# A hybrid SSD and gated-DeltaNet block on one core: kept decays, paired merges, reordered SSD chunks, and difference blocks made between products

## The chip, the cores and the metric

The kernel runs on 1 core of one Trainium2 chip. The metric is device time in microseconds of one execution (lower is better). The profile is one further execution, taken by the hardware profiler.

## The reference

The input x (1024 tokens of 1024 channels) gets 16 meta tokens ahead of it. One layer follows, in float32:

```python
h = h + hybrid_mixer(rmsnorm(h, mix_norm_w), ...)       # two token mixers side by side
h = h + swiglu(rmsnorm(h, ffn_norm_w), w_gate_up, w_down)
return rmsnorm(h, final_norm_w)[:, N_META:]
```

- `hybrid_mixer` projects with `w_in` to 13,376 columns. A causal convolution over 4 tokens and a SiLU make the inputs of the mixers.
- Mixer 1, Mamba-2 SSD: 32 heads of 64 channels in 4 groups, state 128. Per chunk: `scores = (C B^T) * exp(cumulative decay differences)`, `y = scores @ (x*dt) + decayed old state`, and a new state.
- Mixer 2, gated DeltaNet: 8 query/key heads, 16 value heads of 128. Per chunk: keys `k`, `a_low = strict lower part of (beta k k^T) * decay`, `t_inv = (I + a_low)^-1`, `v_new = u - w @ S`, `o = q_dec @ S + (q k^T * decay) @ v_new`, and a new state `S`.
- Both outputs are normed, gated (`silu(z)`), projected with `w_branch`, weighted by sigmoid gates, summed and projected with `w_out`.
- `swiglu` is `(silu(u @ Wg) * (u @ Wu)) @ Wd` with 2816 inner columns.

## The kernel before

Activations lie channels by tokens, 128 channels on the partitions. Every dense product is made of three matmuls in a reduced float32 format: each operand is split into a high and a low half (a copy on ScalarE, a subtraction on VectorE), and high x high, high x low and low x high are summed in PSUM (`dense`, L138 to L143; `product`, L1000 to L1004). `load_w` (L130 to L136) loads a weight tile into `wraw` (SyncE's queue), and splits it into `whi` and `wlo`; all three have two buffers. `weights(name)` (L192) loads one tile ahead, in the order of `proj_order`.

Stage 1, to about 80 us: norm of the input, decays of all heads (`cum`, `rowD`, `rowS`).

Stage 2, DeltaNet, to about 1090 us: eight head pairs (`NSUB`), one query/key head and two value heads each, chunks of 128 tokens, and a chunk of the 16 meta tokens (c = 8). Per pair i:
- `dn_conv(i)`: four weight tiles (q, k, v, v), convolution, and `squares` (L441): transposes of q and k to PSUM and a square with a sum on ScalarE, for the norms.
- `dn_p1(i, c)`: key-key product, `decay` (two broadcast matmuls L420, two Relu, one Exp), and the matrix `N` into `W`; `W` goes to DRAM in blocks of 32.
- `dn_inv(i)`: VectorE inverts all 32 x 32 diagonal blocks at once (60 operations), DMAs bring them back into `W`, transposed copies go to `T32`.
- `dn_merge(i, c)`: three steps of small matmuls (32 x 32, 32 x 64, 64 x 64 of the array; L567, L568, L574, L578) with copies between them join the blocks to the inverse of 128.
- `dn_p2(i, c)`: the recurrence. It makes `decay` a second time (L612), the query-key product (L610) and the transposed keys (L611), then the products with the state.
- Between them lie the z tiles of pair i - 1 and gate tiles: dense matmuls, 11 us each.

Stage 3, SSD, to about 1770 us: per group nine chunks (`ssd_chunk`, L690), spread over the weight tiles of the next group. Stage 4, to about 2160 us: branch products (`load_y`, `tile_`). Stage 5: `w_out`, then the FFN by a scheme with seven products instead of eight blocks: `head` (L1011) makes two of a tile's products, the loop over j (L1085) five, of sums and differences of weight blocks (`comb`, on GpSimd) with the blocks t1, t2, t3, 22, t4 of the normed activations. t1 to t4 and 22 are made ahead of the loop (L1066 to L1081). Then the down products and the final norm.

What sets the order: the text of the program gives priorities. A planner orders each engine's instructions when the program is built, from modelled durations, so dense matmuls of later tiles stand between the small ones of DeltaNet. Each engine then runs its list in that order and waits where an operand is not ready.

Of the kernel before, what the change touches and what calls it, by code (L numbers as in the profile page):

```python
# [20 lines left out]
NT = 1024  # L21
NM = 16
# [70 lines left out]
def body(tc, A):  # L93
# [35 lines left out]

    def load_w(src, kk=KD, room=None):  # L130
# [97 lines left out]
    convp = tkp.tile([128, len(CONV), 5], F32, name="convp")  # L228
    cvp = tc.tile_pool(name="cv", bufs=2)
# [201 lines left out]
    T32 = sb.tile([128, 16, 96], F32, name="T32", bufs=1)  # L431
    pool.memset(T32, 0.0)
    sub = [dict() for _ in range(NSUB)]

    def dn_conv(i):
        d = sub[i]
        qk = d["qk"] = sba.tile([128, 2, TT], F32, name="qk")
        ss = sb.tile([128, 2, 9], F32, name="ss")
        pool.memset(ss, 1.0)

        def squares(j):  # L441

            for cc in (range(4), range(4, 8), (8,)):
                ps = psm("z")
                for c in cc:
                    c0, L = cr(c)
                    pv = ps[0:L, 128 * (c % 4):128 * (c % 4) + 128]
                    pe.transpose(pv, qk[:, j, c0:c0 + L], ident)  # L448
                    act.activation(pv, pv, AF.Square, accum_out=ss[0:L, j, c:c + 1])
# [51 lines left out]
    def dn_p1(i, c):  # L501
        d = sub[i]
        c0, L = cr(c)
        if c == 8:
            d["W"] = sb.tile([128, 8, 2, 128], F32, name="W")
            d["Wm"] = sb.tile([NM, 2, NM], F32, name="Wm")
        kT = d["qk"][:, 1, c0:c0 + L]
        ps = psm("p")
        E = sb.tile([128, 2, 128], F32, name="E")
        pe.matmul(ps[0:L, 256:256 + L], kT, kT, start=True, stop=True)  # L510
        decay(E, ps, rowD, selD, 32, (2 * i, 2 * i + 1), c)
        kkm = sb.tile([128, 128], F32, name="kkm")
        dve.tensor_tensor(kkm[0:L, 0:L], ps[0:L, 256:256 + L], stri[0:L, 0:L], op=ALU.mult)
        N = d["W"][:, c] if c < 8 else d["Wm"]
        for h in range(2):
            dve.scalar_tensor_tensor(N[0:L, h], E[0:L, h, 0:L], d["w"][0:L, c, h:h + 1], kkm[0:L, 0:L],
                                     op0=ALU.mult, op1=ALU.mult)
        nd = nd_dram[i]
        if c in (3, 7):
            for b in range(4):  # L520
                r = slice(32 * b, 32 * b + 32)
                for h in range(2):
                    sp.dma_start(V(nd[0:64], "(c h b) s l -> s c h b l", h=2, b=4)[:, c - 3:c + 1, h, b],
                                 d["W"][r, c - 3:c + 1, h, r])
# [3 lines left out]
    def dn_inv(i):  # L528

        d = sub[i]  # L530
        X = sb.tile([66, 32, 32], F32, name="X", bufs=1)
# [18 lines left out]
        for b in range(3):  # L550
            r = slice(32 * b, 32 * b + 32)
            dve.transpose(T32[r, :, r], V(d["W"][r, :, :, r], "s c h l -> s (c h) l"))

    def dn_merge(i, c):

        d = sub[i]
        W = d["W"]
        ps = psm("p")
        zz = sb.tile([128, 2, 3, 32], F32, name="zz")
        p10 = sb.tile([64, 2, 32], F32, name="p10")  # L560
        z4 = V(ps[:, 0:192], "p (h b s) -> p h b s", h=2, b=3)
        for h in range(2):
            pe.matmul(ps[:, 96 * h:96 * h + 96], W[:, c, h], T32[:, 2 * c + h], start=True, stop=True)  # L563
        act.copy(zz, z4)
        p4 = V(ps[:, 192:256], "p (h s) -> p h s", h=2)
        for h in range(2):
            pe.matmul(p4[0:32, h], zz[32:64, h, 0], W[32:64, c, h, 32:64], start=True, stop=True)  # L567
            pe.matmul(p4[64:96, h], zz[96:128, h, 2], W[96:128, c, h, 96:128], start=True, stop=True)  # L568
            dve.transpose(p10[32:64, h], p4[0:32, h])
        act.copy(W[0:32, c, :, 32:64], p4[0:32])  # L570
        act.copy(W[64:96, c, :, 96:128], p4[64:96])
        p5 = V(ps[:, 256:320], "p (h s) -> p h s", h=2)
        for h in range(2):
            pe.matmul(p5[64:128, h], W[32:64, c, h, 64:128], p10[32:64, h], start=True, stop=True)  # L574
        dve.tensor_tensor(zz[64:128, :, 0], zz[64:128, :, 0], p5[64:128], op=ALU.add)
        p6 = V(ps[:, 320:448], "p (h s) -> p h s", h=2)
        for h in range(2):
            pe.matmul(p6[0:64, h], V(zz[64:128, h, 0:2], "p b s -> p (b s)"), W[64:128, c, h, 64:128],  # L578
                      start=True, stop=True)
        act.copy(W[0:64, c, :, 64:128], p6[0:64])  # L580

    def dn_meta(i):
        d = sub[i]
        kT = d["qk"][:, 1, 0:NM]
        ps = psm("a")
        pe.transpose(ps[0:NM, 0:128], kT, ident)
# [3 lines left out]
        kt = sb.tile([128, 128], F32, name="kt")  # L590
        vd = sb.tile([128, 2, 128], F32, name="vd")
        act.copy(kt[0:NM], ps[0:NM, 0:128])
# [3 lines left out]
        pe.matmul(ps[:, 0:256], kt[0:NM], V(vd[0:NM], "p h k -> p (h k)"), start=True, stop=True)  # L596
# [3 lines left out]
    def dn_p2(i, c):  # L600
# [3 lines left out]
        S, v, W = d["S"], d["v"], d["W"]  # L604
# [3 lines left out]
        ps = psm("b")  # L608
        E = sb.tile([128, 2, 128], F32, name="E2")
# [3 lines left out]
        qkm = sb.tile([128, 128], F32, name="qkm")  # L613
        kt = sb.tile([128, 128], F32, name="kt")
# [15 lines left out]
        for h in range(2):  # L630
            pe.matmul(pv[:, 128 * h:128 * h + 128], W[:, c, h], R[:, h], start=True, stop=True)  # L631
# [58 lines left out]
    def ssd_chunk(g, c):  # L690
# [17 lines left out]
        Bl = sb2.tile([128, 128], F32R, name="Bl")  # L708
        act.copy(Bh[0:L], ps[0:L, 0:128])
        dve.tensor_tensor(Bl[0:L], ps[0:L, 0:128], Bh[0:L], op=ALU.subtract)  # L710
        xh = sb2.tile([128, 512], F32R, name="xh", bufs=2)
        xl = sb2.tile([128, 512], F32R, name="xl", bufs=2)
        split(xh[0:L], xl[0:L], xde[0:L], dve)
        pst = psm("a")
        pe.matmul(pst, Bh[0:L], xh[0:L], start=True, stop=False)
        pe.matmul(pst, Bl[0:L], xh[0:L], start=False, stop=False)
        pe.matmul(pst, Bh[0:L], xl[0:L], start=False, stop=True)
        if c == 8:
            S = d["S"] = sb2.tile([128, 512], F32, name="Ss")
            act.copy(S, pst)  # L720
            return
        pe.matmul(ps[:, 128:256], Bc, Cc, start=True, stop=True)
        cbm = sb2.tile([128, 128], F32, name="cbm")
        dve.tensor_tensor(cbm, ps[:, 128:256], tri, op=ALU.mult)
        ec = sb2.tile([128, 4, 128], F32, name="ec")
        E = [sb2.tile([128, 4, 128], F32, name="Es", bufs=3) for _ in range(2)]
        for q in range(2):
# [6 lines left out]
            dve.tensor_tensor(E[q], E[q], cbm.unsqueeze(1).broadcast_to([128, 4, 128]), op=ALU.mult)  # L734
        S = d["S"]
# [68 lines left out]
    for i in range(NSUB):  # L804
# [136 lines left out]

    def sumsq(pl, sm, m, cs):
# [4 lines left out]
        q = pl.tile([128, 512], F32, name="sq")  # L947
# [47 lines left out]
    def raw_w(src, i):  # L995
        r = wp.tile([128, KD, 128], F32, name="wraw", bufs=2)
# [69 lines left out]
    for k in range(4):  # L1066
        norm(k, h2, rs2)
        dve.tensor_tensor(h[k][:, h1], h[k][:, h2], h[k][:, h1], op=ALU.subtract)
        put("t1", k, h[k][:, h1])
    for k in range(4):  # L1070
        norm(k + 4, h2, rs2)
        dve.tensor_tensor(h[k][:, h1], h[k + 4][:, h2], h[k][:, h1], op=ALU.subtract)
        put("t2", k, h[k][:, h1])
    for k in range(4):
        dve.tensor_tensor(h[k][:, h2], h[k + 4][:, h2], h[k][:, h2], op=ALU.subtract)
        put("t3", k, h[k][:, h2])
    for k in range(4):
# [162 lines left out]
```

## Time and profile before

| | |
|---|---|
| three runs | 2960.52, 2960.96, 2972.54 us (median 2960.96) |
| profiled execution | 2960.07 us; span from first to last instruction 2958.4 us |
| TensorE matmul (PE) | 2900.6 us busy, 98% |
| TensorE weight load (PEld) | 2442.0 us, 83% |
| VectorE (DVE) | 1971.9 us, 67% |
| ScalarE (ACT) | 1293.4 us, 44% |
| GpSimd (POOL) | 184.8 us, 6% |
| mean granted TensorE clock | 0.990 of full speed |

A matmul's end is modelled and matmuls overlap, so its own duration (0.39 us for 512 columns) is not what it costs; the distance to the next start is. L142 is a line of the kernel. "[0.24 <-issue]" behind a row is the engine's idle time ahead of it and what ended it.

### The profile page before, as it was taken

To read this page: it belongs to the slowest core of one execution; us is meant where nothing else is said; L and a number is where in the kernel's file an instruction comes from. 1 tells how busy PE (TensorE), PEld (TensorE's weight loads), DVE (VectorE), ACT (ScalarE), POOL (GpSimd) and SP (SyncE) were. 2 spreads that over 40 slices of the span, in tenths; PEclk is the share of its full clock that TensorE was granted. 3 is DMA by queue.
4 is the path that set the end of the run, shared out by engine and by line. 5 is a ranking of instruction groups with operands and counts; after the bars stand their busy time and mean duration, and the time that the engine had idled before them with its cause. 6 is when DMAs were issued, how large, how long until landed. Compare 5 with 4: busy or idle time off the path is not lost.

```text
span 2958.4 us, 42844 instructions
## 1 busy us (share of the span) xinstructions
PE 2900.6 (98%) x16121; PEld 2442.0 (83%) x16121; DVE 1971.9 (67%) x3882; ACT 1293.4 (44%) x3240; POOL 184.8 (6%) x193
## 2 busy tenths in 40 slices
PE   8999999999999999999999999999997999999997
PEld 7888888888888889979888778888876788888886
DVE  7678687787786755767777753564768655556446
ACT  5645545546456353545555544122234233333213
POOL 1000000000000000000000000000101432230000
PEclk9999999999999999999999999999998999999998
DMA  3111121120111201011111124352442222226212
GB/s 114 51 51 44 41 61 44 37 65 27 53 58 30 93 29 51 30 67 47 51 45 45 68 76 154 106 178 90 135 160 86 102 83 86 86 85 224 90 54 75
DMA packets 119255, 227.33 MB, mean 77 GB/s; under 512 B 47064, under 2 KB 53880, under 8 KB 119048
## 3 DMA queue, kind: packets, MB, share of 16 engines
q1 hardware_dynamic: 117320, 222.50, 22.7%
q8 instruction: 127, 2.08, 0.3%
q10 hardware_dynamic: 1728, 2.10, 0.2%
q14 instruction: 80, 0.66, 0.1%
HBM read 175.16 MB, written 49.38 MB: 76 GB/s over the span
## 4 chain that ended last, share of the span: by engine, by line
PE 91%; DVE 4%; DMA 2%; issue 1%; ACT 1%; POOL 1%; SPq 0%; DVEq 0%; ACTq 0%; POOLq 0%
PE psd L142 16%; PE psd L141 16%; PE psd L143 16%; PE pq_p L1002 1%; PE pq_p L1003 1%; PE ps_o L748 1%; PE pq_p L1004 1%; PE ps_p L563 1%; PE pq_psd L1002 1%; PE ps_o L641 1%; PE ps_z L448 1%; PE pq_psd L1003 1%; PE pq_psd L1004 1%; PE ps_a L631 1%; PE ps_b L738 1%
## 5 line engine op out<-in xcount | busy, mean ns | idle before, releaser
L142 PE MATMUL psd<-u_lo,whi 128*128 128x512 f32 (+3 forms) x2136 | 766.2, 359 | 3.7 <-DVE u_lo L150 2.7
L141 PE MATMUL psd<-u_hi,whi 128*128 128x512 f32 (+3 forms) x2136 | 761.1, 356 | 0.0
L143 PE MATMUL psd<-u_hi,wlo 128*128 128x512 f32 (+3 forms) x2136 | 754.9, 354 | 0.7 <-DVE wlo L135 0.7
L134 ACT CAST whi<-wraw 128x1024 fp32r<-128x1024 f32 (+2 forms) x197 | 188.0, 954 | 634.8 <-PE psd L142 454.3
L142 PEld LDWEIGHTS psd<-u_lo,whi 128*128 128x128 f32 x2136 | 406.2, 190 | 40.5 <-issue 5.1
L143 PEld LDWEIGHTS psd<-u_hi,wlo 128*128 128x128 f32 x2136 | 403.9, 189 | 33.0 <-issue 3.3
L141 PEld LDWEIGHTS psd<-u_hi,whi 128*128 128x128 f32 x2136 | 402.6, 189 | 34.6 <-issue 4.2
L135 DVE TENSOR_TENSOR wlo<-wraw,whi 128x1024 fp32r<-128x1024 f32 (+2 forms) x197 | 217.8, 1106 | 138.8 <-ACT whi L134 129.5
L143 PE MATMUL psd<-blk,wlo 128*128 128x512 f32 x512 | 199.4, 389 | 0.8 <-DVE wlo L135 0.8
L141 PE MATMUL psd<-blk,whi 128*128 128x512 f32 x512 | 199.2, 389 | 0.0
L142 PE MATMUL psd<-blk,whi 128*128 128x512 f32 x512 | 199.2, 389 | 0.0
L143 PEld LDWEIGHTS psd<-blk,wlo 128*128 128x128 f32 x512 | 96.1, 188 | 21.6 <-DVE wlo L135 1.7
L141 PEld LDWEIGHTS psd<-blk,whi 128*128 128x128 f32 x512 | 96.1, 188 | 20.0
L142 PEld LDWEIGHTS psd<-blk,whi 128*128 128x128 f32 x512 | 96.1, 188 | 19.8
L908 DVE TENSOR_TENSOR part<-part,psd 128x512 f32<-128x512 f32 x96 | 65.5, 683 | 70.2 <-PE psd L143 70.2
L378 ACT COPY raw<-psd 128x256 f32<-128x256 f32 x165 | 73.4, 445 | 81.9 <-PE psd L143 80.1
L379 POOL MEMSET raw<- 128x3 f32 x56 | 6.3, 113 | 1393.0 <-DVE qk L384 537.1
L986 POOL TENSOR_TENSOR sw<-wraw 128x512 f32<-128x512 f32 x44 | 69.3, 1575 | 353.1 <-DMA wraw<-w_gu 345.1
L702 DVE TENSOR_TENSOR xdt<-ps_z,dtb 128x512 f32<-128x512 f32 (+1 forms) x36 | 24.8, 690 | 89.0 <-PE ps_z L699 89.0
L539 DVE TENSOR_TENSOR itmp<-X 66x30 f32<-66x30 f32 (+14 forms) x240 | 78.2, 326 | 6.3 <-DMA X<-nd 0.8
L541 DVE TENSOR_TENSOR X<-X,itmp 66x30 f32<-66x30 f32 (+14 forms) x240 | 78.3, 326 | 5.9
L423 ACT ACTIVATE Es<-ps_p,cum 128x128 f32<-128x128 f32 x256 | 75.4, 371 | 11.0 <-PE ps_p L420 10.9
(678 smaller groups left out, 6145.3 us busy)
## 6 DMA issues: line engine op xcount, KB each, us to landing
wraw<-w_in SPq DMA_DIRECT2D x105, 512.0 KB, 3.3
wraw<-w_gu SPq DMA_DIRECT2D x48, 512.0 KB, 3.3
wraw<-w_br SPq DMA_DIRECT2D x36, 512.0 KB, 3.4
c<-hc SPq DMA_DIRECT2D x22, 512.0 KB, 2.6
hc<-c SPq DMA_DIRECT2D x22, 512.0 KB, 5.7
wraw<-w_dn SPq DMA_DIRECT2D x40, 256.0 KB, 2.6
g<-zt SPq DMA_DIRECT2D x32, 256.0 KB, 2.0
y_d<-zt SPq DMA_DIRECT2D x32, 256.0 KB, 2.1
```

What stands on the lines that cost most here:

```text
L134: act.copy(hi[:, 0:kk], raw[:, 0:kk])
L135: dve.tensor_tensor(lo[:, 0:kk], raw[:, 0:kk], hi[:, 0:kk], op=ALU.subtract)
L141: pe.matmul(ps[:, 0:n], hi[:, wk0 + k], ahi(k), start=(k == 0), stop=False)
L142: pe.matmul(ps[:, 0:n], hi[:, wk0 + k], alo(k), start=False, stop=False)
L143: pe.matmul(ps[:, 0:n], lo[:, wk0 + k], ahi(k), start=False, stop=(k == kk - 1))
L378: dense_u((name, lambda ps, p0, p1: act.copy(raw[:, 3 + p0:3 + p1], ps)))
L423: act.activation(E[0:L, i, 0:L], ps[0:L, 128 * i:128 * i + L], AF.Relu, bias=cum[0:L, c, h0 + h:h0 + h + 1], scale=-1.0)
L539: dve.tensor_tensor(t, X[:, 0:j, j:j + 1].broadcast_to([66, j, m]), X[:, j:j + 1, j + 1:32].broadcast_to([66, j, m]), op=ALU.mult)
L541: dve.tensor_tensor(X[:, 0:j, j + 1:32], X[:, 0:j, j + 1:32], t, op=ALU.add)
L908: dve.tensor_tensor(part[:, m, cs], part[:, m, cs], ps, op=ALU.add)
L986: pool.tensor_tensor(t, x, y, op=op)
L1002: pe.matmul(ps, w[0][:, k], y[0][:, k], start=start and k == 0, stop=False, skip_group_check=not start)
```

## The change

1. DeltaNet, decays kept: `dn_p1` also makes the query-key product, and `E` (decay times masked query-key) is kept for all eight chunks (`bufs=8`); `dn_p2` makes neither decay, nor that product, nor the transposed keys. The keys are copied out of the transposes of `squares` (two copies of four chunks, `kt`), and `squares` makes a group's transposes first and its squares behind them.
2. DeltaNet, paired merges: `dn_merge` joins two chunks at once (four heads per step). `W` becomes two halves of four chunks (three buffers), its blocks return with 16 DMAs instead of 8; `T32` shares a buffer with `X` and is cleared in each pair.
3. SSD chunks: B, C and the decays first, then x; the state products and the new state behind the y products.
4. `wraw` has one buffer up to the end of the SSD stage (pool `wr1`), then two (`wr2`).
5. FFN: each of the five blocks is made just ahead of the first product that uses it; for j = 0 `comb` runs on VectorE.
6. End: the last norm's scaling is one VectorE operation per tile for all columns; output DMAs go by SyncE's queue, but for odd tiles of the last columns; the squares have two buffers.

```diff
-        raw = wp.tile([128, KD, 128], F32, name="wraw", bufs=2)
+        raw = raws[0].tile([128, KD, 128], F32, name="wraw")
...
                 for c in cc:
-                    pe.transpose(pv, qk[:, j, c0:c0 + L], ident)
-                    act.activation(pv, pv, AF.Square, accum_out=ss[0:L, j, c:c + 1])
+                    pe.transpose(pv(c), qk[:, j, c0:c0 + L], ident)
+                if j == 1 and len(cc) > 1:
+                    d["kt", cc[0] // 4] = kt = sb.tile([128, 4, 128], F32, name="kt", bufs=3)
+                    act.copy(kt, V(ps, "p (c k) -> p c k", c=4))
...
+                for c in cc:
+                    act.activation(pv(c), pv(c), AF.Square, accum_out=ss[0:cr(c)[1], j, c:c + 1])
...
-        ps = psm("p")
+        ps = psm("pb"[c % 2])
         pe.matmul(ps[0:L, 256:256 + L], kT, kT, start=True, stop=True)
+        if c < 8:
+            pe.matmul(ps[:, 384:512], kT, qT, start=True, stop=True)
+            E = d["E", c] = sb.tile([128, 2, 128], F32, name="E", bufs=8)
...
+            dve.tensor_tensor(qkm, ps[:, 384:512], tri, op=ALU.mult)
...
+            dve.tensor_tensor(E, E, qkm.unsqueeze(1).broadcast_to([128, 2, 128]), op=ALU.mult)
...
-                sp.dma_start(d["W"][r, :, h, r], bv(xd_dram[i])[:, :, h, b])
+                for k in range(2):
+                    sp.dma_start(d["W"][k][r, :, h, r], bv(xd_dram[i])[:, 4 * k:4 * k + 4, h, b])
...
+        ch = [(c + h // 2, h % 2) for h in range(4)]
+        for h, (k, e) in enumerate(ch):
+            pe.matmul(ps[:, 96 * h:96 * h + 96], W[:, k, e], T32[:, 2 * k + e], start=True, stop=True)
+        act.copy(zz, V(ps[:, 0:384], "p (h b s) -> p h b s", h=4, b=3))
...
+        dve.transpose(V(p10[32:64], "p h s -> p (h s)"), ps[0:32, 384:512])
...
-        pe.matmul(ps[:, 256:384], kT, qT, start=True, stop=True)
-        pe.transpose(ps[:, 384:512], kT, ident)
-        decay(E, ps, rowD, selD, 32, (2 * i, 2 * i + 1), c)
-        dve.tensor_tensor(qkm, ps[:, 256:384], tri, op=ALU.mult)
-        act.copy(kt, ps[:, 384:512])
-        dve.tensor_tensor(E, E, qkm.unsqueeze(1).broadcast_to([128, 2, 128]), op=ALU.mult)
+        E, kt = d.pop(("E", c)), d["kt", c // 4][:, c % 4]
...
+        x, xdt, xh, xl = inputs()          # ssd_chunk: behind both decay tiles
         S = d["S"]
...
+        pst = states(xh, xl)               # behind the y products
         dve.tensor_tensor(t1, t1, j4(py), op=ALU.add)
+        S2 = d["S"] = sb2.tile([128, 512], F32, name="Ss")
+        dve.tensor_tensor(h8(S2), h8(S), bc(clast), op=ALU.mult)
+        dve.tensor_tensor(S2, S2, pst, op=ALU.add)
...
+    def block_product(ps, w, y, start):
+        if blocks:
+            blocks.pop(0)()
...
+        product(ps, w, Y[y], start, True)
...
+        eng = pool if j else dve
...
-            product(pc, parts(s1, slot()), Y["t1"], True, True)
+            block_product(pc, parts(s1, slot()), "t1", True)
...
-                    if c == 512:
-                        dve.scalar_tensor_tensor(x, x, finw[:, k:k + 1], rs, op0=ALU.mult, op1=ALU.mult)
-                    else:
-                        act.activation(x, x, AF.Copy, scale=finw[:, k:k + 1])
-                        (pool if k % 3 == 1 else dve).tensor_tensor(x, x, rs, op=ALU.mult)
-                    (sp, act)[k // 2 % 2].dma_start(A["out"][:, k, cs], x)
+                    dve.scalar_tensor_tensor(x, x, finw[:, k:k + 1], rs, op0=ALU.mult, op1=ALU.mult)
+                    (act if cs.stop == NT and k % 2 else sp).dma_start(A["out"][:, k, cs], x)
```

## Rows read from the trace of the kernel before

**Rows 1.** Busy by window: PE, PEld, DVE, ACT, POOL, clock, DMA share, GB/s.

```profile
80.00:1090.00 1010.00, 1008.57 (x6477) 854.23 (x6476) 760.76 (x2083) 546.34 (x1812) 14.50 (x49) 0.99 0.16 49
...
261.00:303.00 42.00, 42.00 (x245) 36.70 (x244) 39.59 (x96) 19.57 (x54) 0.42 (x4) 1.00 0.16 54
```

**Rows 2.** Timeline of TensorE in DeltaNet: start, duration, line, shape, count.

```profile
566.80 0.39 PE L631 MATMUL ps_a<-v,W 128*128 128x128 f32 x2
567.11 0.65 PE L574 MATMUL ps_p<-p,W 32*64 32x32 f32 x8
567.69 0.49 PE L610 MATMUL ps_b<-qk 128*128 128x128 f32 x2
568.01 0.27 PE L611 MATMUL ps_b<-ident,qk 128*128 128x128 f32 x1
568.12 0.28 PE L420 MATMUL ps_b<-rowD,selD 96*128 96x128 bf16 x2
568.21 0.48 PE L142 MATMUL psd<-u_lo,whi 128*128 128x512 f32 x1
568.52 0.39 PE L143 MATMUL psd<-u_hi,wlo 128*128 128x512 f32 x1
568.75 0.38 PE L641 MATMUL ps_o<-v,E 128*128 128x128 f32 x2
```

**Rows 3.** Timeline of TensorE: first and last of the 211 merge visits.

```profile
196.32 0.21 PE L567 MATMUL ps_p<-W,zz 32*32 32x32 f32 x1
...
1074.15 0.44 PE L578 MATMUL ps_p<-W,zz 64*64 64x64 f32 x4
```

**Rows 4.** Timeline of TensorE: a transpose of the squares between dense matmuls.

```profile
272.07 0.33 PE L448 MATMUL ps_z<-ident,qk 128*128 128x128 f32 x1
272.15 0.42 PE L142 MATMUL psd<-u_lo,whi 128*128 128x384 f32 x1
272.41 0.34 PE L143 MATMUL psd<-u_hi,wlo 128*128 128x384 f32 x1
272.59 0.33 PE L141 MATMUL psd<-u_hi,whi 128*128 128x384 f32 x1
```

**Rows 5.** Waits: who for whom, us in total, times, longest.

```profile
PEld ps_z L448 <- ACT ps_z L449: 23.8, 99, 0.4
```

**Rows 6.** Timeline of TensorE: first and last of the 57 y visits.

```profile
1198.01 0.66 PE L748 MATMUL ps_o<-Es,xdt 128*64 128x128 f32 x8
...
1737.44 0.66 PE L748 MATMUL ps_o<-Es,xdt 128*64 128x128 f32 x8
```

**Rows 7.** VectorE's groups in DeltaNet: count, busy us, mean ns, idle before.

```profile
L617 DVE TENSOR_TENSOR E<-E,qkm 128x256 f32<-128x256 f32 x64 | 26.8, 419 | 2.0 <-ACT E L426 0.7
...
L615 DVE TENSOR_TENSOR qkm<-ps_b,tri 128x128 f32<-128x128 f32 x64 | 18.4, 287 | 4.9 <-ACT E L423 4.1
```

**Rows 8.** One line's instructions: duration ns min, median, max.

```profile
L548 SPq DMA_DIRECT2D W<-xd x64: 318/448/644, 187.7 to 1029.7; - x64
```

**Rows 9.** Timeline of TensorE where the FFN starts.

```profile
2288.78 0.80 PE L1004 MATMUL pq_psd<-tx,ws_wr 128*128 128x512 f32 x1 [10.33 <-DVE ws_wr L992]
...
2309.16 0.63 PE L1004 MATMUL pq_p<-tx,ws_whi 128*128 128x512 f32 x1
```

**Rows 10.** Timeline of VectorE where the FFN starts.

```profile
2252.45 3.35 DVE L186 RECIPROCAL rs<-rs 128x512 f32<-128x512 f32 x1 [0.70 <-ACT rs L185]
...
2279.61 4.29 DVE L150 TENSOR_TENSOR blk<-hc,blk 128x512 fp32r<-128x512 f32 x7
```

**Rows 11.** Timeline of ScalarE at the end.

```profile
2941.44 0.42 ACT L948 ACTIVATE sq<-hc 128x256 f32<-128x256 f32 x1 [3.78 <-DMA out<-hc]
```

**Rows 12.** Timeline of SyncE's queue: three weight loads.

```profile
1120.20 23.06 SPq L133 DMA_DIRECT2D wraw<-w_in  x3
```

**Rows 13.** Timeline of ScalarE: the split that follows.

```profile
1129.23 1.05 ACT L134 CAST whi<-wraw 128x1024 fp32r<-128x1024 f32 x1 [3.03 <-PE psd L142]
```

**Rows 14.** DMA issues of the page: count, KB each, us to landing.

```profile
wraw<-w_in SPq DMA_DIRECT2D x105, 512.0 KB, 3.3
```

More of the change, by code (lines that the diff above doesn't have):

```diff
@@ L437, in dn_conv @@
         qk = d["qk"] = sba.tile([128, 2, TT], F32, name="qk")
+        d["ktm"] = sb.tile([NM, 128], F32, name="ktm")
         ss = sb.tile([128, 2, 9], F32, name="ss")
@@ L554, in dn_merge @@
+        pool.memset(T32, 0.0)
+        for k in range(2):
+            for b in range(3):
+                r = slice(32 * b, 32 * b + 32)
+                dve.transpose(T32[r, 8 * k:8 * k + 8, r], V(d["W"][k][r, :, :, r], "s c h l -> s (c h) l"))
     def dn_merge(i, c):
         d = sub[i]
-        W = d["W"]
+        W, T32 = d["W"][c // 4], d["T32"]
+        T32 = T32[:, 8 * (c // 4):8 * (c // 4) + 8]
+        c = c % 4
+        ch = [(c + h // 2, h % 2) for h in range(4)]
         ps = psm("p")
-        zz = sb.tile([128, 2, 3, 32], F32, name="zz")
@@ L560, in dn_merge @@
[L560 to L574, printed above, removed]
+        zz = sb.tile([128, 4, 3, 32], F32, name="zz")
+        p10 = sb.tile([64, 4, 32], F32, name="p10")
+        for h, (k, e) in enumerate(ch):
+            pe.matmul(ps[:, 96 * h:96 * h + 96], W[:, k, e], T32[:, 2 * k + e], start=True, stop=True)
@@ new lines, in dn_merge @@
+        act.copy(zz, V(ps[:, 0:384], "p (h b s) -> p h b s", h=4, b=3))
+        c4 = lambda t: V(t, "p (k e) s -> p k e s", e=2)
+        p4 = V(ps[:, 384:512], "p (h s) -> p h s", h=4)
+        for h, (k, e) in enumerate(ch):
+            pe.matmul(p4[0:32, h], zz[32:64, h, 0], W[32:64, k, e, 32:64], start=True, stop=True)
+            pe.matmul(p4[64:96, h], zz[96:128, h, 2], W[96:128, k, e, 96:128], start=True, stop=True)
+        dve.transpose(V(p10[32:64], "p h s -> p (h s)"), ps[0:32, 384:512])
@@ L575, in dn_merge @@
+        act.copy(W[0:32, c:c + 2, :, 32:64], c4(p4[0:32]))
+        act.copy(W[64:96, c:c + 2, :, 96:128], c4(p4[64:96]))
+        ps = psm("p")
+        p5 = V(ps[:, 0:128], "p (h s) -> p h s", h=4)
+        for h, (k, e) in enumerate(ch):
+            pe.matmul(p5[64:128, h], W[32:64, k, e, 64:128], p10[32:64, h], start=True, stop=True)
         dve.tensor_tensor(zz[64:128, :, 0], zz[64:128, :, 0], p5[64:128], op=ALU.add)
-        p6 = V(ps[:, 320:448], "p (h s) -> p h s", h=2)
-        for h in range(2):
-            pe.matmul(p6[0:64, h], V(zz[64:128, h, 0:2], "p b s -> p (b s)"), W[64:128, c, h, 64:128],
+        p6 = V(ps[:, 128:384], "p (h s) -> p h s", h=4)
@@ L579, in dn_merge @@
+        for h, (k, e) in enumerate(ch):
+            pe.matmul(p6[0:64, h], V(zz[64:128, h, 0:2], "p b s -> p (b s)"), W[64:128, k, e, 64:128],
                       start=True, stop=True)
-        act.copy(W[0:64, c, :, 64:128], p6[0:64])
+        act.copy(W[0:64, c:c + 2, :, 64:128], c4(p6[0:64]))
     def dn_meta(i):
         d = sub[i]
-        kT = d["qk"][:, 1, 0:NM]
         ps = psm("a")
-        pe.transpose(ps[0:NM, 0:128], kT, ident)
         for h in range(2):
@@ L589, in dn_meta @@
                       start=True, stop=True)
-        kt = sb.tile([128, 128], F32, name="kt")
+        kt = d["ktm"]
         vd = sb.tile([128, 2, 128], F32, name="vd")
-        act.copy(kt[0:NM], ps[0:NM, 0:128])
         dve.tensor_tensor(vd[0:NM], V(ps[0:NM, 128:384], "p (h k) -> p h k", h=2),
@@ L595, in dn_meta @@
         ps = psm("a")
-        pe.matmul(ps[:, 0:256], kt[0:NM], V(vd[0:NM], "p h k -> p (h k)"), start=True, stop=True)
+        pe.matmul(ps[:, 0:256], kt, V(vd[0:NM], "p h k -> p (h k)"), start=True, stop=True)
         S = d["S"] = sb.tile([128, 2, 128], F32, name="S", bufs=3)
@@ L630, in dn_p2 @@
         for h in range(2):
-            pe.matmul(pv[:, 128 * h:128 * h + 128], W[:, c, h], R[:, h], start=True, stop=True)
+            pe.matmul(pv[:, 128 * h:128 * h + 128], W[:, h], R[:, h], start=True, stop=True)
         vd = sb.tile([128, 2, 128], F32, name="vd")
@@ L995, in raw_w @@
     def raw_w(src, i):
[L996 removed]
+        r = raws[0].tile([128, KD, 128], F32, name="wraw")
         sp.dma_start(r, src)
```

154 lines of the change are left out of this document (87 added, 67 removed).

## The prediction

> **What bounds the kernel now.** I read the busy shares of the page's table first: TensorE is at 98%, so a change has to take time out of TensorE's own stream, or out of the few places where that stream stands still. The windows say where it stands [rows 1]: in the DeltaNet stage (80 to 1090 us) it idles 1.4 us of 1010. But a busy matmul is a modelled one, so the third view, the matmuls in order of time, is read for the distance from one start to the next [rows 2]. The matmul of 512 columns at 568.52 costs 0.23 us; the one before it, of the same size, costs 0.31, because other work ran just ahead of it. Such small losses are what the change can reach in the first two stages. In the window of an inverse VectorE is full as well, busy 39.59 of 42 us [rows 1], which comes back as a rival. Real idle time stands in two short places: where the FFN starts (10.33 us ahead of one matmul, [rows 9]) and at the very end.
>
> **DeltaNet: kept decays.** Each of the 64 steps (8 head pairs, 8 chunks) loses one transpose and two decay broadcasts on TensorE. In [rows 2] the transpose L611 takes 568.12 - 568.01 = 0.11 us, the two broadcasts L420 568.21 - 568.12 = 0.09. So 64 x 0.20 = 12.8, and the eight meta transposes, at the same 0.11, make 0.9: 13.7 us. The query-key product moves to the first pass and costs the same there. It stood in a visit of its own; without the visit the dense matmul behind no longer pays its 0.31 - 0.23 = 0.08. 64 x 0.08 is 5; as some visits lie against other work of the same chunk, I take 3 (0 to 5). ScalarE loses two Relu, an Exp and a copy per chunk; it isn't the bound, so nothing is counted.
>
> **DeltaNet: squares.** Today a key or query transpose waits until ScalarE has squared the one before, in the same bank: 99 such waits [rows 5]. In [rows 4] the dense matmul behind one costs 0.26, the next, of the same size, 0.18. With four transposes in a row only the last one's follower pays: 96 of 128 followers x 0.08 = 8, and of each wait as much again at most. I take 10 (0 to 14).
>
> The Trainium skill (TensorEngine Tiling (Array Packing), Key Properties) says that changing the tiling mode drains TensorE, and that changing the tile alone does not. Full-size transposes change no mode, so by that rule this term would be nil and the sum 10 us smaller; the row shows a loss without a change of mode, and I go by the row.
>
> **DeltaNet: paired merges.** The matmuls stay the same in number; what halves is how often the array goes from full size to small tiles and back. In [rows 2] the two full-size L631, 0.11 each as L611, take 0.31 to the first small one: going in costs 0.09. Behind the eight small L574 the two L610 take 0.32 instead of 0.22: 0.10. That is 0.19 a visit, and what the way out takes itself, which these rows don't separate. I counted the uninterrupted visits of lines 567 to 578 in the timeline: 211, from the first to the last of [rows 3]. Paired, three steps in 32 pairs make 96; the planner now splits some of its 192, so I expect about 110. 100 visits fewer x 0.18 (some touch each other) = 18 us. Bounds: 5 if half the pairs are split again, 27 if each visit saved 0.27.
>
> What it costs: the second pass waits for both chunks' merge, while the four heads' transposes on VectorE become one. Dense matmuls lie beside it; if they run out, that is the third rival.
>
> DeltaNet together: 13.7 + 3 + 10 + 18 = 45 us.
>
> **SSD order.** Decays first, then x. Today the y products of a chunk come in two visits of eight instructions, 57 visits for 32 chunks [rows 6]. With both decay tiles ready before x, one visit per chunk: 25 fewer, at 0.19 and some way out, 0.26: 7 us. The state products move behind y and the new state behind them; the next chunk wants it only a tile later. Bounds -3 (the state comes late) to 10.
>
> **FFN start.** Today VectorE makes all five difference blocks before the first product can end: TensorE waits 10.33 us until 2288.78, and the five products of j=0 end at 2309.16 + 0.4 [rows 9], 20.8 us for 60 matmuls that need 60 x 0.23 = 13.8, as GpSimd is late with the combinations. Afterwards j=0 is paced by VectorE's list: from the reciprocal's end, 2252.45 + 3.35 = 2255.8, 44 block operations (12, 12, 8, 4, 8) and about 15 others (low halves, combinations, additions) at 4.29 / 7 = 0.61 us [rows 10]: 59 x 0.61 = 36, to 2291.8; the last product ends 12 x 0.23 = 2.8 later, 2294.6. Gain 15 us. Bounds: 4 if most blocks are still placed first (of the 7 us lost on GpSimd some are saved), 22 if combinations and halves run before the reciprocal ends.
>
> **End.** ScalarE sat 3.78 us behind output DMAs that it issues itself and that wait for VectorE [rows 11], and it scales a tile between two squares. Both go; one VectorE operation with both factors replaces the work of two or three engines. I take 3 (1 to 5).
>
> **One raw buffer for w_in.** The next tile's load now waits until the tile before is split. Today's load starts then already: at 1120.20 [rows 12] a load is issued, the next split starts at 1129.23 [rows 13], 9 us later; landing takes 3.3 [rows 14]. Hidden with 5.7 us to spare: cost 0, at the start of the kernel up to one landing, 3.3. With that cover gone a tile would cost 3.3 us.
>
> The Trainium skill (Trainium Kernel Development and Optimization, Best Practices) asks for double buffers, so that DMA and compute overlap. By that rule the 103 later tiles would pay their 3.3 us, 340 in all, and the time would be 3230; in the rows above the overlap comes from the split halves, which keep two buffers, so I give that 1 in 100.
>
> **Sum.** 45 + 7 + 15 + 3 = 70 us, from the profiled execution's 2960.07 (span 2958.4, and 1.7 around it): 2890. The median of the runs, 2960.96, is 1 us from it, so the same number stands. All low ends: 13.7 + 0 + 0 + 5 - 3 + 4 + 1 - 3 = 18, time 2942; all high ends: 13.7 + 5 + 14 + 27 + 10 + 22 + 5 = 97, time 2863.
>
> **Rivals.**
> 1. *The visits are split as before.* The order on each engine is the planner's, and it makes 57 y visits of a possible 32 today. Merges and y then give nothing: 2890 + 18 + 7 = 2915. For it: [rows 6]; against it: all operands of a paired step come ready with one copy. 0.17.
> 2. *The FFN blocks still come first,* as VectorE's list is ordered before it runs: 2890 + 11 = 2901. Against it: each block now stands behind the halves of its own product. 0.15.
> 3. *The chain of dependences governs DeltaNet (the slower side).* An inverse cannot start before the first pass is done, and that pass gets two more VectorE products per chunk, 0.287 + 0.419 us [rows 7], 64 x 0.706 = 45 us; behind the inverse 64 more DMAs are issued, 0.448 each [rows 8], 29 us. If no dense matmuls are left to lie beside them, 74 us come on top, nothing of DeltaNet's 45 is gained, and the time is 2960 + 74 - 7 - 15 - 3 = 3009. It decides once the dense work runs out inside a head pair. For it: VectorE full during the inverse. Against it: TensorE idles 1.4 us in the whole stage, so dense work has lasted everywhere, and the second pass is rid of the same two products. 0.05.
> 4. *Half of it:* DeltaNet's saved TensorE time becomes time only by half, as VectorE is full beside it: 2890 + 22 = 2912. 0.15.
>
> My forecast, all terms within their bounds: 0.45; mixtures of 1, 2 and 4, near 2945: 0.02; the single buffer 0.01. About 0.5%, 15 us, is what a measurement can tell from no change. Slower by more: 0.06 (rival 3 and the single buffer). Within: 0.04, the mixtures and the worst of rival 4. Faster: 0.90, all the rest. Range 2862 to 2930: below it lies more than all high ends, above it rival 3, the mixtures and the worst ends of 1 and 4.
>
> **What would show it.** L420 gone from the second pass; merge visits near 110 and y visits near 32; few waits of TensorE's weight loads for the squares; j=0 of the FFN done 15 us sooner after the reciprocal than today; no wait of ScalarE for output DMAs. I am wrong if TensorE shows waits of a microsecond and more inside DeltaNet, or if the splits of w_in wait for a DMA.

## The result and the profile after

The changed kernel takes 2935.72 us (median of 4 runs, 2933.44 to 2938.23) against 2961.86 for the one before: a ratio of 0.9904, 95% interval 0.988 to 0.9929. The sign is the forecast one, the size is not: 26 us came where 70 were forecast, and 2935.7 lies above the range.

The span of the profiled executions fell by 24.6 us, from 2958.4 to 2933.8. By stage, cut at the starts of four TensorE instructions that both kernels have (last products of the second pass, last SSD norm transpose, first and last FFN product):

| stage | before | after | gain | forecast |
|---|---|---|---|---|
| start and DeltaNet | 1088.8 | 1081.1 | 7.6 | 45 |
| SSD | 706.3 | 702.5 | 3.9 | 7 |
| branch and w_out | 452.0 | 451.2 | 0.8 | 0 |
| FFN | 446.1 | 438.3 | 7.9 | 15 |
| down and end | 265.2 | 260.7 | 4.4 | 3 |

DeltaNet hands over more than its end says: dense w_in matmuls worth 638.2 us (each counted at its undisturbed price, 0.23 us for 512 columns) are done by then, against 630.4. So DeltaNet gained 7.6 + 7.8 = 15.4 us, and SSD, which finds 7.8 us less to do, lost 4.

The windows of the changed kernel (busy us and count of PE, PEld, DVE, ACT, POOL, then clock, DMA share, GB/s) answer to [rows 1]: all of DeltaNet, its last 161 us, and a stretch inside them.

```profile
80.00:1081.00 1001.00, 964.77 (x6310) 841.29 (x6309) 733.09 (x1979) 464.08 (x1446) 24.51 (x56) 0.99 0.17 50
920.00:1081.00 161.00, 144.84 (x935) 116.95 (x934) 98.63 (x311) 61.90 (x216) 2.37 (x3) 0.95 0.15 47
943.00:992.00 49.00, 32.84 (x223) 25.48 (x222) 36.57 (x140) 24.09 (x99) 0.94 (x1) 0.89 0.09 23
```

Before, TensorE idled 1.4 us of 1010 here. Now it idles 36 of 1001, and 16 of the 49 us from 943 to 992, where the timeline has no dense matmul between these two:

```profile
948.31 0.39 PE L145 MATMUL psd<-u_hi,wlo 128*128 128x512 f32 x1
992.41 0.78 PE L143 MATMUL psd<-u_hi,whi 128*128 128x512 f32 x1
```

No other engine is full there. The waits of TensorE in DeltaNet (who for whom, us in total, times, longest) answer to [rows 5]:

```profile
PE psd L143 <- ACT raw L382: 10.2, 15, 1.7
PE ps_z L692 <- DVE zt L402: 6.9, 3, 4.5
PE ps_o L661 <- ACT v L657: 3.8, 5, 1.0
PE ps_b L524 <- DVE rs_to L163: 2.3, 1, 2.3
...
PEld ps_z L454 <- ACT ps_z L461: 10.3, 24, 0.8
```

The 99 waits for the squares are 24. The others hardly occurred before. Most are waits for a step of the DeltaNet chain; the largest, 10.2 us, is dense products that wait until ScalarE has copied an earlier product out of their bank.

What holds the chain is seen by following one head pair. Timeline of the changed kernel, the instructions that release one another from one pair's chunk 3 to the next pair's chunk 3:

```profile
468.48 0.63 PE L659 MATMUL ps_a<-vd,kt 128*128 128x256 f32 x2
469.15 0.59 ACT L457 COPY kt<-ps_z 128x512 f32<-128x512 f32 x1
474.64 0.25 ACT L461 ACTIVATE ps_z<-ps_z 16x128 f32<-16x128 f32 x1
481.76 0.17 DVE L477 TENSOR_TENSOR w<-dtb,ss 128x18 f32<-128x18 f32 x1
483.93 0.59 DVE L538 SCALAR_TENSOR_TENSOR W<-E,w,kkm 128x128 f32<-128x128 f32 x2
492.23 10.77 SPq L547 DMA_DIRECT2D nd<-W  x16
504.19 0.46 SPq L557 DMA_DIRECT2D X<-nd  x1
509.49 0.19 DVE L563 TENSOR_TENSOR itmp<-X 66x30 f32<-66x30 f32 x1
550.90 0.18 DVE L565 TENSOR_TENSOR X<-X,itmp 66x30 f32<-66x30 f32 x1
554.10 7.44 SPq L573 DMA_DIRECT2D W<-xd  x16
562.90 0.35 PE L593 MATMUL ps_p<-T,W 128*128 128x96 f32 x2
590.34 0.63 PE L659 MATMUL ps_a<-vd,kt 128*128 128x256 f32 x2
591.01 0.58 ACT L457 COPY kt<-ps_z 128x512 f32<-128x512 f32 x1
```

The kept transposed keys have three buffers of four chunks; a pair needs two. The second half of the next pair's keys can be copied out (469.15) only after the last product with the first half of the present pair's (468.48, chunk 3). The squares are taken in the same bank behind that copy, so the norms (w, 481.76), the first products of W, the inverse (509.49 to 551.08), the merges (562.90) and the next chunk 3 (590.34) all come behind it. The loop closes after 121.9 us. In all seven pairs that have one before them, the second half is copied out within 0.4 us of that product, in six of them 0.04 us behind it.

Dense work fills the holes and runs ahead, until beside the first pass of the last pair none is left that may start. Timeline of ScalarE there, and one row of VectorE:

```profile
909.49 0.60 ACT L399 ACTIVATE zt<-psd 128x512 f32<-128x512 f32 x1 [3.60 <-PE psd L145]
915.77 0.59 ACT L399 ACTIVATE zt<-psd 128x512 f32<-128x512 f32 x1
920.61 0.60 ACT L399 ACTIVATE zt<-psd 128x512 f32<-128x512 f32 x1 [4.25 <-PE psd L145]
984.27 0.74 DVE L402 SCALAR_TENSOR_TENSOR zt<-zt,dnw,ps_z 128x512 f32<-128x512 f32 x1
989.99 0.60 ACT L399 ACTIVATE zt<-psd 128x512 f32<-128x512 f32 x1 [8.30 <-DMA y_d<-zt]
```

The three z buffers are full from 921 on with z tiles of the seventh pair, which wait for that pair's second pass, and the two banks of the dense products keep the two results behind them. It isn't that no dense work remains: tiles of w_in are left for all of the SSD stage, but there is no room to put a result.

Pair lengths, from the start of one pair's last product to the next one's, us (runs of the next section included):

| | 1 | 2 | 3 | 4 | 5 | 6 | 7 |
|---|---|---|---|---|---|---|---|
| before | 122.5 | 119.5 | 116.2 | 114.9 | 129.2 | 115.2 | 123.8 |
| after | 124.9 | 121.2 | 122.9 | 119.8 | 123.0 | 119.8 | 105.9 |
| after, ballast on TensorE | 119.7 | 114.4 | 119.1 | 118.4 | 117.0 | 114.8 | 122.1 |
| four key buffers | 119.0 | 114.1 | 115.5 | 111.3 | 111.5 | 104.7 | 116.1 |
| keys made again, 2 buffers | 122.4 | 121.1 | 122.5 | 124.0 | 120.3 | 119.8 | 104.1 |
| keys made again, 8 buffers | 118.9 | 112.8 | 110.5 | 105.5 | 128.3 | 113.6 | 125.2 |
| four key buffers, single merges | 124.1 | 121.9 | 122.5 | 126.0 | 122.1 | 127.2 | 107.0 |

The row of before is uneven, which fits a stage that TensorE's stream sets; that of after stays within about 5 us up to the sixth, which fits a loop.

In the SSD stage the y products (line 777) answer to [rows 6]. Timeline of TensorE, one chunk, dense matmuls left out:

```profile
1371.47 0.66 PE L777 MATMUL ps_o<-Es,xdt 128*64 128x128 f32 x8
1372.46 0.50 PE L746 MATMUL ps_a<-xh,Bh 128*128 128x512 f32 x1 [0.33 <-ACT xh L148]
1372.80 0.40 PE L747 MATMUL ps_a<-xh,Bl 128*128 128x512 f32 x1
1374.00 0.66 PE L777 MATMUL ps_o<-Es,xdt 128*64 128x128 f32 x8
```

Still two visits of eight instructions: 61 visits in all, 57 before. The first half starts when the first decay tile is ready, the second comes 2.5 us later. And the state products, now behind y, wait for ScalarE's split of x in 14 of the 36 chunks, 4.3 us in all.

Where the FFN starts (answers to [rows 9, 10]), first VectorE, then TensorE:

```profile
2240.16 3.35 DVE L188 RECIPROCAL rs<-rs 128x512 f32<-128x512 f32 x1 [0.70 <-ACT rs L187]
```

```profile
2276.72 0.76 PE L1038 MATMUL pq_p<-tx,ws_whi 128*128 128x512 f32 x1 [3.54 <-DVE hc L1166]
2283.07 0.80 PE L1038 MATMUL pq_p<-tx,ws_whi 128*128 128x512 f32 x1 [3.46 <-ACT tx L148]
...
2285.67 0.63 PE L1040 MATMUL pq_p<-tx,ws_whi 128*128 128x512 f32 x1
```

The wait of 10.33 us of [rows 9] is gone; two of 3.5 stand here. Before, there was a second one too, 15 us behind the first:

```profile
2304.31 0.79 PE L1002 MATMUL pq_p<-tx,ws_whi 128*128 128x512 f32 x1 [3.68 <-DVE hc L1111]
2304.90 0.63 PE L1003 MATMUL pq_p<-tx,ws_whi 128*128 128x512 f32 x1
```

j=0 ends at 2286.3, 42.8 us after the reciprocal's end (2243.5); before it was 54.0.

### The profile page after: what moved, and what is told of

Its sections match the earlier page's. It is cut to its first block, busy times and chain, and to the rows that moved or that the text cites. A ratio compares the mean times of both kernels' runs of the same rounds, so it can differ in the third digit from the quotient of the medians.

```text
span 2933.8 us, 41854 instructions
## 1 busy us (share of the span) xinstructions
PE 2848.0 (97%) x15921; PEld 2420.8 (83%) x15921; DVE 1938.7 (66%) x3788; ACT 1203.0 (41%) x2856; POOL 180.4 (6%) x190
## 4 chain that ended last, share of the span: by engine, by line
PE 83%; ACT 7%; DVE 6%; DMA 3%; issue 1%; SPq 0%; POOL 0%; DVEq 0%; POOLq 0%; ACTq 0%
PE psd L143 15%; PE psd L144 15%; PE psd L145 15%; PE pq_p L1038 1%; PE pq_p L1039 1%; PE pq_p L1040 1%; ACT Es L427 1%; PE ps_p L593 1%; PE pq_psd L1040 1%; PE pq_psd L1039 1%; PE pq_psd L1038 1%; PE ps_a L639 1%; PE ps_a L651 1%; PE ps_o L661 1%; PE ps_o L777 1%
## 5 line engine op out<-in xcount | busy, mean ns | idle before, releaser
L143 PE MATMUL psd<-u_hi,whi 128*128 128x512 f32 (+3 forms) x2136 | 759.8, 356 | 10.7 <-ACT raw L382 10.2
L144 PE MATMUL psd<-u_lo,whi 128*128 128x512 f32 (+3 forms) x2136 | 755.1, 354 | 3.7 <-DVE u_lo L152 2.7
L1022 POOL TENSOR_TENSOR sw<-wraw 128x512 f32<-128x512 f32 x42 | 63.3, 1507 | 377.3 <-DMA wraw<-w_gu 377.3
L399 ACT ACTIVATE zt<-psd 128x512 f32<-128x512 f32 x64 | 38.1, 596 | 88.4 <-PE psd L145 66.1
L725 DVE TENSOR_TENSOR cbm<-ps_p,tri 128x128 f32<-128x128 f32 x32 | 9.3, 291 | 87.2 <-PE ps_p L723 87.0
```

The lines of the kernel that those rows point to most:

```text
L143: pe.matmul(ps[:, 0:n], hi[:, wk0 + k], ahi(k), start=(k == 0), stop=False)
L144: pe.matmul(ps[:, 0:n], hi[:, wk0 + k], alo(k), start=False, stop=False)
L1022: eng.tensor_tensor(t, x, y, op=op)
```

## Experiments

Three theories. L: a loop of dependences paces DeltaNet, closed by the third key buffer. E: the loop is closed by the eight buffers of the kept decays. S: TensorE's stream sets the time, and the saving was never there.

**Four key buffers.** Room for the fourth buffer came from three small moves.

```diff
-  kt = sb.tile([128, 4, 128], F32, name="kt", bufs=3)
+  kt = sb.tile([128, 4, 128], F32, name="kt", bufs=4)
-  tmp = sb.tile([66, 256], F32, name="itmp", bufs=1)
+  tmp = xx[0:66, 1024:1280]      # unused end of the buffer of X
-  d["ktm"] = sb.tile([NM, 128], F32, name="ktm")
+  d["ktm"] = sb.tile([NM, 128], F32, name="ktm", bufs=1)
-  p10 = sb.tile([64, 4, 32], F32, name="p10")
+  p10 = sb.tile([64, 4, 32], F32, name="p10", bufs=1)
```

(`xx` is the whole buffer of which `X` is a view.)

> The changed kernel with four buffers instead of three for the kept transposed keys (room for it: the inverse's scratch moved into the unused end of the shared X/T32 buffer, one buffer instead of two for ktm and p10). Theory L (loop): a pair's second half of keys cannot be copied out until the pair before has passed its chunk 3, so its norms, its first pass and its inverse all start behind that; the loop of about 121 us per pair paces DeltaNet and the dense work runs out in the last pair. Then with four buffers the key squares of the next pair end some 50 us earlier, TensorE's idle time between 80 and 1081 us falls from 32 to under 15 us, and the time is 2905 to 2925 (after: 2935.7). Theory E (the eight buffers of the kept decays are the tie): squares earlier, but pairs stay at 119 to 123 us and the time at 2930 to 2940. Theory S (TensorE's own stream sets the time, the saving never existed): 2933 to 2938.

Measured: 2899.41 us, ratio 0.9774 (0.9754 to 0.9793), 36 us below the changed kernel and 6 below the least that L expected. Timeline of the same pair, as above:

```profile
402.69 0.59 ACT L457 COPY kt<-ps_z 128x512 f32<-128x512 f32 x1
406.80 0.59 ACT L457 COPY kt<-ps_z 128x512 f32<-128x512 f32 x1 [0.74 <-PE ps_z L454]
438.98 0.17 DVE L477 TENSOR_TENSOR w<-dtb,ss 128x18 f32<-128x18 f32 x1
456.65 0.61 DVE L538 SCALAR_TENSOR_TENSOR W<-E,w,kkm 128x128 f32<-128x128 f32 x2 [0.34 <-ACT E L430]
```

Both halves are copied out within 4 us, and the first W product starts 27 us earlier. Windows of this kernel:

```profile
80.00:1037.00 957.00, 944.95 (x6249) 827.18 (x6248) 736.14 (x1977) 469.92 (x1443) 25.12 (x56) 0.99 0.17 51
```

DeltaNet ends at 1036.8, TensorE idles 12 us instead of 36. With 626.8 us of dense work done by then, DeltaNet has gained 52.0 - 3.6 = 48.4 us on the kernel before: the 45 of the forecast and 3 more. Pairs take 104 to 119 us. L stands, E and S fall.

The traces answer E apart as well. In the changed kernel each of the eight buffers of kept decays has been read 3.9 us or more before the next pair writes it. With four key buffers the next pair writes at once; timeline of this run, TensorE and then ScalarE:

```profile
472.91 0.38 PE L662 MATMUL ps_o<-v,E 128*128 128x128 f32 x2
473.33 0.63 ACT L427 ACTIVATE E<-ps_p,cum 128x128 f32<-128x128 f32 x2 [0.26 <-PE ps_o L662]
```

In six of seven pairs two to four of the eight writes start 0.04 us behind that product. So the kept decays are the next resource over which the loop closes.

**Only the room for it** (the three moves, still three key buffers).

> The changed kernel with the three buffer moves of the run with four key buffers (inverse's scratch in the shared X/T32 buffer, one buffer for ktm, one for p10) but still three buffers for the kept keys. Theory L (the third key buffer is the tie): as the changed kernel, 2930 to 2941, key squares of a pair still ending some 25 us before its first pass ends. Rival (one of the three moves made the gain): 2895 to 2910.

Measured: 2937.88, ratio 0.9909 (0.9884 to 0.9933), as the changed kernel. The gain is the fourth buffer's.

**Ballast on TensorE, after and before.**

```diff
-  for i, h in enumerate(hs):
+  for i, h in list(enumerate(hs)) * (3 if h0 else 1):     # h0 is 0 in the SSD stage
       pe.matmul(ps[0:L, 128 * i:128 * i + L], sel..., row...)
```

In the kernel before, an argument of `decay` that only the first pass sets does the same.

> The changed kernel with a ballast on TensorE alone: in DeltaNet's first pass each pair of decay broadcasts is issued three times instead of once, with the same result. 72 steps x 2 extra pairs x 0.09 us = 13 us of TensorE time. Theories L and E (a chain of dependences paces DeltaNet, TensorE has idle time there): 0 to 5 us of it show, 2934 to 2941. Theory S: 2935.7 + 13 = 2949, give or take 3.

> The kernel before with the same ballast in its first pass (13 us of TensorE time). All theories of mine say that TensorE's stream bounds this kernel: 2961.9 + 13 = 2975, give or take 3. Rival (the kernel before stood on the chain of dependences too, and TensorE was only busy on paper): 2960 to 2966.

Measured: after with ballast 2936.52, ratio 0.99 (0.9879 to 0.992): 13 us more of TensorE's time cost 0.8. So TensorE did not bound DeltaNet any more, and S falls a second time. The test isn't a pure one: the planner makes another order, and pairs take 114 to 122 us in it. The loop still closes over the same buffer (0.04 us from product to copy in six of seven pairs), so its length of 121.9 us belongs to one order and is no constant.

Before with ballast 2969.60, ratio 1.0026 (1.0009 to 1.0042), 3 to 12 us: some of it shows, but the median lies between both expectations. The mean granted clock of each run settles it. The 17 runs of before beside it go from 2955.8 us at 0.992 to 2974.3 at 0.985. At 0.991 two of them took 2957.9 and 2958.6, and seven with ballast 2967.6 to 2970.4: 11 of the 13 us show, so TensorE's stream did bound the kernel before. At 0.990 the ballast costs the changed kernel 1 to 6 us (2936.5 to 2941.7 against 2935.6 and 2935.8).

**Ballast with four key buffers.**

> Four key buffers and the ballast of 13 us on TensorE in the first pass, which cost the changed kernel 0.8 us (2935.7 to 2936.5). If TensorE's stream bounds DeltaNet again: 2899.4 + 13 less the 8 us of idle time left there, so 2904 to 2913. If a chain still paces it: 2899 to 2903.

Measured: 2913.06, ratio 0.9821 (0.9798 to 0.9844): 13.7 us more, at the same mean clock of 0.993. With the loop cut, TensorE's stream bounds the stage again.

**Keys made again in the second pass,** with two and with eight buffers.

```diff
-  E, kt = d.pop(("E", c)), d["kt", c // 4][:, c % 4]
+  E = d.pop(("E", c))
+  ps = psm("b")
+  pe.transpose(ps[:, 384:512], kT, ident)
+  kt = sb.tile([128, 128], F32, name="kt")            # then: bufs=8
+  act.copy(kt, ps[:, 384:512])
```

The two copies of four chunks in `squares` go.

> The changed kernel, with the transposed keys of the eight chunks no longer kept but made again in the second pass, as before the change; the meta chunk's stay kept. That puts 64 transposes of 0.11 us back on TensorE (7 us) and 64 small copies on ScalarE, and takes the buffer of kept keys away. Theory L: the loop is cut, so the time does not rise by the 7 us; 2912 to 2935. Theory E: pairs stay at about 121 us and the 7 us lie in holes: 2934 to 2942. Theory S: 2935.7 + 7 = 2943, give or take 2.

> The kernel that makes the transposed keys again in the second pass, now with eight small buffers for them instead of two. In the run with two, bank b stayed with the second pass until its last key copy, which waited for a key buffer, and the odd chunks of the next first pass, which want the same bank, came 11 us later. Theory L, wider: it is any buffer that the second pass gives back late and the next first pass needs, so with eight the keys are copied out early, bank b comes free, pairs fall from 121 to some 115 us and the time is 2900 to 2918 (2899.4 of the four-buffer run, 7 us of transposes). Rival (keeping the keys is itself what helps; making them again costs the loop): 2930 to 2940.

Measured: 2936.96 with two buffers (0.9905, 0.9881 to 0.9929), 2925.69 with eight (0.9866, 0.9841 to 0.9892). The first missed L's mark and lies where E was expected. But E is not the cause: the kept decays' buffers are free about 3 us or more before they are written. The squares end early (413 us instead of 475), yet pairs still take 121 us. Its timeline of TensorE shows why:

```profile
476.58 0.33 PE L636 MATMUL ps_b<-ident,qk 128*128 128x128 f32 x1
482.32 0.49 PE L521 MATMUL ps_b<-qk 128*128 128x128 f32 x2
```

and ScalarE's, between the two:

```profile
482.00 0.27 ACT L638 COPY kt<-ps_b 128x128 f32<-128x128 f32 x1 [0.42 <-PE ps_a L660]
```

The next first pass (line 521, odd chunks in bank b) comes only once the second pass has done with that bank, and the second pass's last key copy there, at 482.00, waited until a product (line 660) gave back one of two key buffers. The loop had closed over another resource. With eight buffers pairs 2 to 4 fall to 105 to 113 us, as expected; the time, 2926, misses the expected 2918. Its pairs 5 and 7 take 128 and 125 us. Of the 26 us above the four-buffer run, 7 are the transposes (as priced) and 8 more idle time; the rest I did not separate.

**Merges one chunk at a time, with four key buffers.**

```diff
   for c in range(0, 8, 2):
       dn_merge(i, c)
+      dn_merge(i, c + 1)          # each for one chunk, as before the change
```

> Four key buffers, merges one chunk at a time as before the change. TensorE stands still for 8 us of DeltaNet in the four-buffer run, so what the array loses shows again. Forecast's term: 18 us (5 to 27), so 2899.4 + 18 = 2917. By the traces of before and after (entry, exit and inside of 211 visits 60.9 us, of 112 visits 27.7) it is 33: 2932. Rival (the chain still paces DeltaNet, the merges lie beside it): 2900 to 2906.

Measured: 2961.12, ratio 0.998 (0.9964 to 0.9996): 62 us more (51 in the profiled execution), above every expectation. Timeline of TensorE, first merge of a pair and first product of the next first pass, with single merges:

```profile
439.81 0.58 PE L594 MATMUL ps_p<-T,W 128*128 128x96 f32 x4
...
476.01 0.21 PE L524 MATMUL ps_p<-qk 128*16 128x16 f32 x2
```

and with paired ones:

```profile
427.16 0.35 PE L594 MATMUL ps_p<-T,W 128*128 128x96 f32 x2
...
452.53 0.21 PE L524 MATMUL ps_p<-qk 128*16 128x16 f32 x2
```

36.2 us against 25.4: both use bank p, and the first pass starts when the merges have done with it. That is 10.8 us a pair, in a chain that is long again (pairs of 122 to 127 us up to the sixth). TensorE idles 24 us of DeltaNet instead of 12. By the traces DeltaNet loses 48 us, dense work counted as above, so some 36 are TensorE's own time and 12 the chain's. So pairing is worth more than the array's time: it shortens the loop. That bank p closes it here is read from the trace; I did not test it apart.

**SSD in the order of before, with four key buffers.** The function of the SSD chunk as before the change.

> Four key buffers, SSD chunks in the order of the kernel before. The stage account of the two traces says that the new order gained nothing and cost about 4 us: 2895, 2890 to 2899. The forecast's own term (new order gains 7) would give 2906; the rival of no difference 2899 to 2900.

Measured: 2897.46, ratio 0.9776 (0.9749 to 0.9803), not to be told from 2899.4 by the runs; by the traces the stage is 710.0 us long instead of 714.0, with the same dense work in it. So the new order costs about 4 us in the trace, and the forecast's gain of 7, which would have made 2906, did not come.

**y products with heads 4 to 7 first,** in the new and in the old order.

```diff
-  for h in range(8):
+  for h in (4, 5, 6, 7, 0, 1, 2, 3):
```

> Four key buffers, and the eight y products of an SSD chunk issued with heads 4 to 7 first, whose decays are ready last. The 61 visits of the array in small tiles (58 of eight instructions, as the second half waits some 2 us for the second decay tile) become about 32 of sixteen. At the 0.26 to 0.29 us a visit that the forecast used: 2899.4 - 7.5 = 2892, 2888 to 2896. Rival (the wait for the later decay costs more than the visit, or the planner splits them again): 2898 to 2903.

> Four key buffers, SSD chunks in the order of before (no wait of the state products for xh) and the y products with heads 4 to 7 first (32 visits instead of 57). The run with the old order gives 2897.5, the visits 25 x 0.26 = 6.5 less: 2891, 2887 to 2895. Rival (the old order's y waits again for the later decay): 2896 to 2899.

Measured: 2894.53 in the new order (0.9765, 0.9738 to 0.9791), 2890.76 in the old one (0.9742, 0.9719 to 0.9765). A chunk of the last:

```profile
1334.86 1.09 PE L769 MATMUL ps_o<-Es,xdt 128*64 128x128 f32 x16
...
1350.89 1.09 PE L769 MATMUL ps_o<-Es,xdt 128*64 128x128 f32 x16
```

32 visits of sixteen in both, since the first product now waits for the later decay; both times lie in the expected ranges. The last kernel beats before by 2.6% and the changed kernel by 45 us.

**FFN blocks first, with four key buffers** (and GpSimd for the first combinations).

```diff
-  blocks = [t1, t2, t3, b22, t4]
+  for b in (t1, t2, t3, b22, t4):
+      b()
+  blocks = []
-  eng = pool if j else dve
+  eng = pool
```

> Four key buffers, the five FFN blocks made ahead of the first gate tile and its combinations on GpSimd, as before the change. Forecast's term 15 (4 to 22): 2914. By the stage account of the traces (first to last FFN product 445.7 before, 437.8 after) it is 8: 2907. Rival (the blocks were made first in both): 2899 to 2901.

Measured: 2903.93, ratio 0.9791 (0.9768 to 0.9814), 4.5 us more; the FFN stage is 4.8 us longer in the trace. The edit is worth about 5, at the low end of 4 to 22. The other 3 of the stage's 8 us I did not trace.

## Why the prediction was wrong

The step that failed is the sum for DeltaNet: "45 us" of TensorE's time were taken as 45 us of time. The reason given was "TensorE idles 1.4 us in the whole stage, so dense work has lasted everywhere". That row shows what bound the kernel before, and the ballast agrees. It says nothing of the chain that the change itself makes: the loop over the third key buffer is not in the kernel before. It was never added up; in the changed kernel it is 121.9 us long, and the pairs of before take 120 on average, so no time per pair could be won. TensorE's own stream did get shorter, by about 50 us: the 15.4 that DeltaNet gained and 35 that came back as idle time. So the saving was sized rightly, and the overlap that should have turned it into time was wrong. The prediction named the sign of it, waits of a microsecond and more on TensorE inside DeltaNet, and they are there (up to 4.5 us).

By its own steps:

- *Kept decays, 13.7 + 3.* The instructions went: L420 leaves the second pass, and TensorE's full-size work besides the dense matmuls in DeltaNet, at undisturbed prices, falls from 218.9 to 204.6 us. Right; the 3 for the visits I did not measure apart.
- *Squares, 10.* Waits from 23.8 us to 10.3, and matmuls behind the transposes lose 4.1 us instead of 12.4. Right in mechanism; I did not run it apart. The Trainium skill (TensorEngine Tiling (Array Packing), Key Properties) puts the draining on a change of mode; these followers lost time without one.
- *Merges, 18.* Visits from 211 to 112, forecast 110. Entering, leaving and gaps inside cost 60.9 us before and 27.7 after: 33, above the bound of 27; instructions inside a visit stand closer too. Undersized; and the run with single merges shows a second worth, in the chain, that the step lacked.
- *Rival 3, the chain,* had the right mechanism at 0.05 and the wrong price. It priced VectorE's two products and the 64 DMAs, 74 us. What closed the loop was a buffer count that stands in the diff: three where two pairs in flight need four. The added products and DMAs did not come on top of the pair as priced. The diff also gives the kept decays eight buffers and W three halves; I counted what the kept tiles save and did not ask who gives each back and who waits for it.
- *SSD, 7.* Wrong: the visits stayed at two a chunk, as the two halves start 2.5 us apart though x comes last, and the state products got a wait. Cost 4, beyond the low bound of -3.
- *FFN, 15.* The mechanism was right at first: VectorE is busy 33 of 33 us after the reciprocal. j=0 gained 11 us and the stage 8; by the run on it the blocks' part is 5. What was mis-sized is the end of j=0, forecast 38.8 us after the reciprocal and measured 42.8: two waits of 3.5 us and matmuls 0.43 us apart instead of 0.23, as the last section shows. The prediction put 7 us of the kernel before down to GpSimd. Its trace shows the wait of 3.68 us there, which leads over VectorE and ScalarE back to GpSimd and from there to a weight load, and 22 matmuls at the slower step, an estimated 22 x 0.20 = 4.4 us that the new order doesn't take away.
- *End, 3.* 4.4 with the down stage. Right in size; I did not run it apart.
- *One raw buffer, 0.* Right. The splits of w_in name no load in what they waited for, in either trace. So breaking the Trainium skill's rule for double buffers (Trainium Kernel Development and Optimization, Best Practices) costs nothing here; that the split halves serve as the second buffer is the reading, not tested apart.

With four key buffers the terms by the traces are DeltaNet 48, SSD -4, branch 1, FFN 8, end 5, together 58; the profiled run took 2902.1 and the median is 2899.4, inside the range. The number would have held for a kernel with one buffer more, but partly by luck: the merges are 15 us above their term, SSD 11 and the FFN 7 below.

## What to carry to other kernels

When an engine at 98% is relieved, the next bound can be a loop of dependences, one that the change itself makes, so add one round of it up before counting the saving as time. For each tile that a change keeps longer, write down which instruction gives the buffer back and which one waits for it: the loop closes over the scarcest, be it SBUF or a PSUM bank. Its mark in a trace is a reader and the next writer of one buffer that stand 0.04 us apart in every round. A ballast on the relieved engine that costs next to nothing shows that this engine no longer bounds; one buffer more, with the room for it tested alone, shows what does.

## What the runs showed of the hardware

TensorE's clock had no place in the forecast. In the changed kernel, between the first of the waits of 3.5 us where the FFN starts and the work behind the second, the granted clock stands at the lower of its two levels (0.50, 1.2 GHz). Windows:

```profile
2243.00:2276.00 33.00, 27.68 (x114) 20.31 (x112) 32.95 (x55) 16.79 (x30) 0.23 (x1) 0.99 0.14 48
2277.00:2288.00 11.00, 7.54 (x17) 5.12 (x17) 6.13 (x11) 4.45 (x8) 5.48 (x4) 0.50 0.14 48
2289.00:2313.00 24.00, 23.07 (x102) 18.74 (x100) 14.95 (x17) 6.43 (x11) 11.43 (x8) 1.00 0.31 110
```

A 512-column matmul is then 0.43 us from the next instead of 0.23. For the 17 matmuls of that window this is an estimated 17 x 0.20 = 3.4 us on top of the waits.

The other surprise was SyncE's queue. In the ScalarE wait of 8.30 us shown above, for a z buffer, the tile in it is done at 985.01 (line 402), but its store stands behind sixteen DMAs of the last inverse in program order, which themselves wait for the first pass. It is issued 2.8 us later:

```profile
976.88 10.86 SPq L547 DMA_DIRECT2D nd<-W  x16
987.84 0.85 SPq L695 DMA_DIRECT2D y_d<-zt  x2
```
